# Expert stages: the down products' second round and the release of their buffers placed ahead of the next group's gate products, and the branch hints placed elsewhere

## The chip, the core and the metric

One core of one Trainium2 chip runs one program. Time is device microseconds of one execution; a comparison is made between medians of runs taken on the same chip. Engines are named as in the profile: PE (TensorE matmuls), PEld (TensorE weight loads, issued by the same sequencer), DVE (VectorE), ACT (ScalarE), POOL (GpSimd), SP (SyncE, which here only issues DMAs). A q behind the name (PEq, SPq) is the engine's sequencer.

## What is computed

Two blocks on 256 tokens of width 1024, in float32. The first block has two layers, each an attention (differential attention, then a latent attention called mla) followed by a hierarchical mixture of 64 experts; the second block is a mixer and a gated MLP. The change touches the expert stages alone:

```python
weights = g_w * (e_w / jnp.sum(e_w, axis=-1, keepdims=True))      # two experts per token, of one group of eight
combine = jnp.einsum('tk,tke->te', weights, jax.nn.one_hot(expert_id, N_EXPERTS, dtype=jnp.float32))
def body(e, acc):
    hid = jax.nn.silu(t @ w_gate[e]) * (t @ w_up[e])               # 1024 -> 256, twice
    return acc + combine[:, e, None] * (hid @ w_down[e])           # 256 -> 1024
out = lax.fori_loop(0, N_EXPERTS, body, jnp.zeros_like(t))
```

All 64 experts' weights (three matrices of 1 MB each) are read from HBM once per layer, about 201 MB a layer.

## The kernel before

**Groups.** `moe(i, held)` handles layer i's 64 experts in 16 groups of four. Each expert has 32 slots (CAP). For a group, `gather_half` (L905) picks the tokens of the four experts by products with a one-hot matrix, in two halves; `expand` (L946) makes the gate products ("g") and the up products ("u") of the four experts side by side in one PSUM tile; `hidden` (L959) applies silu and multiplies; `hidden_T` transposes; `down_mm` (L974) makes the down products into two PSUM tiles; `weighted` (L988) scales them by the routing weight and splits them in two parts, on ACT and DVE; `scatter` (L1000) spreads them to the 256 tokens by products with the scatter matrix and DVE adds to x (L1007).

**Overflow.** If an expert of the group has more than 32 tokens, the next 32 are done in a second round: behind `tc.If(n > CAP)` labelled further (L1083) the kernel gathers them and makes their gate and up products, and behind a second `tc.If` labelled beyond (L1047) their down products and scatter (`down_more`, L1009). Inside it stands a further branch for third and later rounds (`rounds`, L1030). In this input that happens in group 1 and group 15 of layer 0 and in group 11 of layer 1. Where it doesn't happen, each engine takes the branch over the body.

**Order on PE.** PE's and SP's programs follow the order of the source (`manual_schedule`); ACT, DVE and POOL are ordered by the framework. In the iteration of group g the source has: down products of group g-1, gate products of g, scatter of g-1, beyond of g-1, release of D (the down weights' buffers) of g-1, up products of g, hidden, further of g, release of the gate and up buffers of g, scatter matrix of g, gather half 0 of g+1, transposes of g's hidden, gather half 1 of g+1. Group 15 is written out behind the loop.

**Hints.** `hint` (L1040) places an instruction on PE's sequencer that names a branch by its label and says it will likely be taken, behind a given product. The hint of beyond g-1 stands behind the last down product of g-1, that of further g behind the first up product of g. The branches of group 15 have none. `at` is the list of the last products, from which the place is taken.

**Buffers.** Class `Regions` has 16 buffers of 1 MB in SBUF. In an expert stage one holds the normalised tokens `h`, so 15 are for weights: 12 of a group and 3 of the next. The weights are loaded by one DMA each, issued by SP in the order gate, up, down (four each) group by group. A release (`reg.done`) lets the next transfers be issued, and they wait on the engines' semaphores for it. A release of D lets one down and three gate transfers go, a release of gate and up the next gate, four up and three down. SP keeps at most eight transfers under way. `reg.want(n)` keeps n buffers free for what follows.

Of the kernel before, what the change touches and what calls it, by code (L numbers as in the profile page):

```python
# [18 lines left out]
P = 128  # L19
# [220 lines left out]
def tile_model(ctx: ExitStack, tc: tile.TileContext, a: dict, out: bass.AP, stop: int = 6):  # L240
# [541 lines left out]
    def moe(i, held):  # L782
# [114 lines left out]

        def one_hot(rks, ov=False):

            gm = view(ov4[0], (T, 4, 32)) if ov else t1((T, 4, 32))  # L900
            for t in range(T):
                V.tensor_tensor(gm[:, t], sl4, rks[:, t, :, None].to_broadcast([P, 4, 32]), op=ALU.is_equal)
            return gm

        def gather_half(gm, xg, hb):  # L905

            pg = sc_ps()
            for k4 in range(4):
                for t in range(T):
                    PE.matmul(pg[:, ts(k4, P)], lhsT=h[:, t, 4 * hb + k4, :], rhs=gm[:, t].rearrange("p a b -> p (a b)"),  # L910
                              start=(t == 0), stop=(t == 1))
            V.tensor_tensor(xg[hb], pg.rearrange("p (k n) -> p k n", k=4),  # L912
                            gain[:, 4 * hb:4 * hb + 4, None].to_broadcast([P, 4, P]), op=ALU.mult)
# [30 lines left out]
        at = []  # L944

# [20 lines left out]
        def hidden_T(hd, ov=False):  # L966
            pt = at_ps()
            for k in range(2):
                PE.transpose(pt[:, ts(k, P)], hd.rearrange("p (q k) -> p k q", k=2)[:, k, :], ident)
            hT2 = view(ov4[1], (2, P)) if ov else t1((2, P))  # L970
            V.tensor_copy(hT2, pt[:, 0:256].rearrange("p (k n) -> p k n", k=2))
            return hT2
# [15 lines left out]
        def weighted(pys, hf, ws, ov=False, tables=False):  # L988
# [5 lines left out]
            ins = split_to(y[0], y[1], pys[hf], ws)  # L994
            if tables:
                with tc.issue_after(ins):
                    exp_log()
# [61 lines left out]
        last = None  # L1059
        with tc.manual_schedule(engines={ET.PE}):  # L1060
            for g in range(15):
                n = nc.values_load(cnt[0:1, g:g + 1], min_val=0, max_val=256) if g else None
                if g:
                    n_, hT2, sc, more = last
                    pys = down_mm(g - 1, hT2)
                    hint("beyond", g - 1, at[-1])
                    ys = [weighted(pys, hf, sc[1]) for hf in range(2)]
                pgu = ad_ps()
                expand(g, "g", pgu, xg)
                if g:  # L1070
                    for hf in range(2):
                        scatter(hf, sc[0], ys[hf])
                    beyond(g - 1, n_, more)
                    done(g - 1, "d")
# [3 lines left out]
                if g:  # L1078
                    hint("further", g, at[0])
# [16 lines left out]
                gather_half(gm, xg, 0)  # L1096
                hT2 = hidden_T(hd)
# [5 lines left out]
            n_, hT2, sc, more = last  # L1103
            pys = down_mm(14, hT2)
            hint("beyond", 14, at[-1])
            ys = [weighted(pys, hf, sc[1]) for hf in range(2)]
            pgu = ad_ps()
            expand(15, "g", pgu, xg)
            for hf in range(2):
                scatter(hf, sc[0], ys[hf])  # L1110
            beyond(14, n_, more)
            done(14, "d")
            pgu_o = mm_ps()
            with tc.If(n > CAP):
                xg_o, sc_o = further(15)
                expand(15, "g", pgu_o, xg_o)
            expand(15, "u", pgu, xg)
            hd = hidden(pgu)
            sc = scatter_matrix(15, gm)
            hT2 = hidden_T(hd)  # L1120
            with tc.If(n > CAP):
                expand(15, "u", pgu_o, xg_o)
                more = (hidden_T(hidden(pgu_o, True), True), sc_o)
            done(15, "g", "u")
            beyond(15, n, more)

            pys = down_mm(15, hT2)
            for hf in range(2):
                scatter(hf, sc[0], weighted(pys, hf, sc[1], tables=hf == 0))
        reg.want((7, 9)[i])  # L1130
        done(15, "d")
# [454 lines left out]
```

## Time and profile before

| what | value |
|---|---|
| median of 3 runs | 1635.39 us (1633.1 to 1638.16) |
| the profiled execution | 1631.57 us |
| its span, first to last instruction | 1629.8 us |
| mean granted TensorE clock | 0.919 |
| PE busy | 1342.7 us, 82% of the span |
| DVE, ACT busy | 691.8 us, 434.5 us |
| DMA | 513.14 MB, mean 315 GB/s |
| expert stages, by their first and last hidden | 170.8 to 638.7 us and 789.3 to 1245.0 us |

The page cuts the span into 40 slices of 40.7 us. In its DMA row a 9 says that the 16 DMA engines were busy 90% or more. PE's busy share counts matmuls whose ends are modelled, and is high in most slices, whether or not PE sets the pace; who waits for whom is read from the waits and the timeline. A sequencer hands instructions out ahead of the engine that runs them, so a branch can stand before the end of the product in front of it. A row of busy time by stretch holds the stretch, its length, then for PE, PEld, DVE, ACT and POOL the busy us and the number of instructions, then the granted clock as a share of full speed, the DMA share and GB/s.

### The profile page before, as it was taken

The numbers are of one execution on the slowest core, as the hardware profiler recorded it, in microseconds if no ns is written. First come the engines' busy times: TensorE is split into PE (matmuls) and PEld (weight loads), VectorE is DVE, ScalarE is ACT, GpSimd is POOL, SyncE is SP. The second block draws the span as 40 slices with busy tenths as digits, with TensorE's granted clock in tenths as the row PEclk, the third lists the DMA queues.
The fourth block names the chain that finished last, engine by engine and source line by source line (L and its number), as shares of the span: only waits on it lengthen the run. The fifth ranks groups of instructions, "written<-read, shape, count | busy, mean of one in ns | idle before, by whom it ended". The sixth has DMA issues, their size and how long they took to land. (4 is left out here: it accounts for less than half of the span.)

```text
span 1629.8 us, 26706 instructions
## 1 busy us (share of the span) xinstructions
PE 1342.7 (82%) x10695; PEld 927.9 (57%) x10695; DVE 691.8 (42%) x1630; ACT 434.5 (27%) x946; POOL 54.1 (3%) x69
## 2 busy tenths in 40 slices
PE   7998987777677777998877677778777899999996
PEld 6766654443354444776643454545442656599996
DVE  6875232222222223775322222222322754477776
ACT  5764010000000001774000000000001543455555
POOL 2100000000000000120000000000000010000001
PEclk9998999889878899999988989899888999999998
DMA  9377889999999998244999999999899764475410
GB/s 365 127 262 322 334 343 419 419 419 418 417 397 416 418 418 337 93 144 167 392 417 403 418 419 418 419 418 393 341 418 379 285 235 159 149 270 189 171 37 27
DMA packets 112810, 513.14 MB, mean 315 GB/s; under 512 B 13955, under 2 KB 41283, under 8 KB 61344
## 3 DMA queue, kind: packets, MB, share of 16 engines
q1 hardware_dynamic: 111296, 508.14, 78.5%
q8 instruction: 160, 2.62, 0.7%
q0 software_dynamic: 1024, 1.41, 0.3%
q14 instruction: 106, 0.87, 0.1%
q10 hardware_dynamic: 224, 0.10, 0.0%
HBM read 508.56 MB, written 1.05 MB: 313 GB/s over the span
## 5 line engine op out<-in xcount | busy, mean ns | idle before, releaser
L955 PE MATMUL ad<-R,t 128*32 128x256 f32 x4352 | 327.0, 421 | 101.4 <-DMA R<-in_moe_w_up_dram 42.2
L955 PEld LDWEIGHTS ad<-R,t 128*32 128x32 f32 x4352 | 171.1, 120 | 260.3 <-issue 87.6
L910 PE MATMUL sc<-t,R 128*128 128x128 f32 x1120 | 176.1, 323 | 18.2 <-issue 12.0
L910 PEld LDWEIGHTS sc<-t,R 128*128 128x128 f32 x1120 | 167.5, 237 | 20.6 <-issue 17.2
L1007 DVE TENSOR_TENSOR x<-x,mm 128x512 f32<-128x512 f32 x140 | 90.0, 684 | 149.0 <-PE mm L1004 149.0
L982 PE MATMUL mm<-R,t 128*32 128x512 f32 x1120 | 135.4, 625 | 9.5 <-PEq L1047 5.0
L961 ACT ACTIVATE t<-ad 128x256 f32<-128x256 f32 x34 | 13.0, 383 | 481.7 <-PE ad L955 481.7
L963 DVE TENSOR_TENSOR t<-t,ad 128x256 f32<-128x256 f32 x34 | 14.3, 421 | 254.4 <-ACT t L961 254.4
L409 ACT ACTIVATE t<-mm,ws 128x512 fp32r<-128x512 f32 x64 | 44.0, 687 | 263.1 <-PE mm L982 263.1
L912 DVE TENSOR_TENSOR t<-sc,ffng 128x512 f32<-128x512 f32 x70 | 48.4, 692 | 134.6 <-PE sc L910 134.6
L400 DVE TENSOR_TENSOR R<-R,R 128x1024 fp32r<-128x1024 f32 (+3 forms) x78 | 93.2, 1198 | 27.4 <-ACT R L399 26.1
L400 DVE TENSOR_TENSOR t<-R,t 128x1024 fp32r<-128x1024 f32 (+3 forms) x76 | 88.7, 1171 | 23.6 <-ACT t L399 23.4
L410 DVE SCALAR_TENSOR_TENSOR t<-mm,ws,t 128x512 fp32r<-128x512 f32 x64 | 48.0, 751 | 104.3 <-ACT t L409 77.5
L399 ACT ACTIVATE R<-R 128x1024 fp32r<-128x1024 f32 (+3 forms) x78 | 78.7, 1014 | 50.8 <-PE ad L417 15.1
L934 PE MATMUL at<-con,t 128*128 128x128 f32 x70 | 16.6, 323 | 85.5 <-PEq L1083 73.9
L1004 PE MATMUL mm<-t,t 128*128 128x512 f32 x256 | 77.6, 422 | 11.1 <-DVE x L1007 10.2
L399 ACT ACTIVATE t<-R 128x1024 fp32r<-128x1024 f32 (+3 forms) x76 | 76.4, 1008 | 37.8 <-PE ad L416 15.3
L982 PEld LDWEIGHTS mm<-R,t 128*32 128x32 f32 x1120 | 35.0, 114 | 82.9 <-issue 77.5
L1004 PEld LDWEIGHTS mm<-t,t 128*128 128x128 f32 x256 | 43.1, 188 | 45.6 <-DVE x L1007 22.8
L934 PEld LDWEIGHTS at<-con,t 128*128 128x128 f32 x70 | 7.9, 155 | 99.7 <-issue 89.5
L415 PE MATMUL mm<-R,R 128*128 128x512 f32 (+3 forms) x139 | 56.4, 408 | 3.3 <-ACT R L399 2.6
L416 PE MATMUL mm<-R,R 128*128 128x512 f32 (+3 forms) x139 | 55.4, 399 | 0.0
(448 smaller groups left out, 2263.8 us busy)
## 6 DMA issues: line engine op xcount, KB each, us to landing
R<-in_moe_w_gate_dram SPq DMA_DIRECT2D x128, 1024.0 KB, 15.2
R<-in_moe_w_up_dram SPq DMA_DIRECT2D x128, 1024.0 KB, 15.8
R<-in_moe_w_down_dram SPq DMA_DIRECT2D x128, 1024.0 KB, 19.8
R<-in_w_ada_dram SPq DMA_DIRECT2D x24, 1024.0 KB, 7.7
R<-in_w_up_dram SPq DMA_DIRECT2D x22, 1024.0 KB, 6.3
R<-in_diff_w_in_dram SPq DMA_DIRECT2D x12, 1024.0 KB, 15.0
R<-in_w_down_dram SPq DMA_DIRECT2D x11, 1024.0 KB, 5.5
R<-in_w_in_dram SPq DMA_DIRECT2D x8, 1024.0 KB, 7.7
```

What stands on the lines that cost most here:

```text
L399: S.activation(hi, w, AF.Copy)
L400: V.tensor_tensor(lo, w, hi.bitcast(F32), op=ALU.subtract)
L409: first = S.activation(hi, src, AF.Copy, scale=scale)
L410: V.scalar_tensor_tensor(lo, src, scale, hi.bitcast(F32), op0=ALU.mult, op1=ALU.subtract)
L415: PE.matmul(acc, lhsT=lt[0], rhs=rt[0], start=start, stop=False, **kw)
L416: PE.matmul(acc, lhsT=lt[0], rhs=rt[1], start=False, stop=False, **kw)
L910: PE.matmul(pg[:, ts(k4, P)], lhsT=h[:, t, 4 * hb + k4, :], rhs=gm[:, t].rearrange("p a b -> p (a b)"), start=(t == 0), stop=(t == 1))
L912: V.tensor_tensor(xg[hb], pg.rearrange("p (k n) -> p k n", k=4), gain[:, 4 * hb:4 * hb + 4, None].to_broadcast([P, 4, P]), op=ALU.mult)
L955: mm = PE.matmul(pgu[32 * j:32 * j + 32, co:co + 256], lhsT=xg[k // 4][:, k % 4, 32 * j:32 * j + 32], rhs=w, start=(k == 0 and co == 0), s ...
L982: mm = PE.matmul(py[32 * j:32 * j + 32, :], lhsT=hT2[:, k, 32 * j:32 * j + 32], rhs=ws[j][:, k, ts(hf, 512)], start=(k == 0), stop=(k == 1))
L1004: PE.matmul(pos[t], lhsT=sc[:, ts(t, P)], rhs=y[part], start=(part == 0), stop=(part == 1))
L1007: V.tensor_tensor(xs, xs, pos[t], op=ALU.add)
```

## The change

In the loop, `down_mm`, `weighted`, `beyond` and the release of D become one function `close(g)`, which stands ahead of the gate products of g+1; the scatter stays behind the gate products. The hint of further g stands behind the last gate product of g, ahead of the scatter. The hint of beyond g stands behind the first half of the gather of g+1. In group 15 the overflow's gather stands ahead of the gate products, its gate and up products both behind hidden, under a branch with a label and a hint; beyond 15 stands behind the first round's down products, and has a hint; the activation table for the next stage (`exp_log`) is loaded ahead of the last scatter and no longer inside `weighted`; `reg.want` stands ahead of the last group's down products.

```diff
--- before.py
+++ after.py
@@ -895,6 +895,9 @@
         ov4 = [t15() for _ in range(4)]
         r2 = sb([P, T, 4], "r2")
 
+
+        at = []
+
         def one_hot(rks, ov=False):
 
             gm = view(ov4[0], (T, 4, 32)) if ov else t1((T, 4, 32))
@@ -907,8 +910,9 @@
             pg = sc_ps()
             for k4 in range(4):
                 for t in range(T):
-                    PE.matmul(pg[:, ts(k4, P)], lhsT=h[:, t, 4 * hb + k4, :], rhs=gm[:, t].rearrange("p a b -> p (a b)"),
-                              start=(t == 0), stop=(t == 1))
+                    mm = PE.matmul(pg[:, ts(k4, P)], lhsT=h[:, t, 4 * hb + k4, :],
+                                   rhs=gm[:, t].rearrange("p a b -> p (a b)"), start=(t == 0), stop=(t == 1))
+            at.append(mm.ins)
             V.tensor_tensor(xg[hb], pg.rearrange("p (k n) -> p k n", k=4),
                             gain[:, 4 * hb:4 * hb + 4, None].to_broadcast([P, 4, P]), op=ALU.mult)
 
@@ -941,8 +945,6 @@
             V.tensor_copy(ws, ptr[:, 256:257])
             return sc, ws
 
-        at = []
-
         def expand(g, nm, pgu, xg):
 
             ws = [reg.get(("moe", i, g, nm, j)) for j in range(4)]
@@ -966,7 +968,8 @@
         def hidden_T(hd, ov=False):
             pt = at_ps()
             for k in range(2):
-                PE.transpose(pt[:, ts(k, P)], hd.rearrange("p (q k) -> p k q", k=2)[:, k, :], ident)
+                mm = PE.transpose(pt[:, ts(k, P)], hd.rearrange("p (q k) -> p k q", k=2)[:, k, :], ident)
+            at.append(mm.ins)
             hT2 = view(ov4[1], (2, P)) if ov else t1((2, P))
             V.tensor_copy(hT2, pt[:, 0:256].rearrange("p (k n) -> p k n", k=2))
             return hT2
@@ -985,16 +988,13 @@
                 pys.append(py)
             return pys
 
-        def weighted(pys, hf, ws, ov=False, tables=False):
+        def weighted(pys, hf, ws, ov=False):
             if ov:
                 y = ovy
             else:
                 room = t4((2, 512), F32R)
                 y = [room[:, 0, :], room[:, 1, :]]
-            ins = split_to(y[0], y[1], pys[hf], ws)
-            if tables:
-                with tc.issue_after(ins):
-                    exp_log()
+            split_to(y[0], y[1], pys[hf], ws)
             return y
 
         def scatter(hf, sc, y):
@@ -1057,26 +1057,30 @@
 
         gm, xg = gather(rk[:, :, 0:4])
         last = None
+
+        def close(g):
+
+            n, hT2, sc, more = last
+            pys = down_mm(g, hT2)
+            ys = [weighted(pys, hf, sc[1]) for hf in range(2)]
+            beyond(g, n, more)
+            done(g, "d")
+            return sc, ys
+
         with tc.manual_schedule(engines={ET.PE}):
             for g in range(15):
                 n = nc.values_load(cnt[0:1, g:g + 1], min_val=0, max_val=256) if g else None
                 if g:
-                    n_, hT2, sc, more = last
-                    pys = down_mm(g - 1, hT2)
-                    hint("beyond", g - 1, at[-1])
-                    ys = [weighted(pys, hf, sc[1]) for hf in range(2)]
+                    sc, ys = close(g - 1)
                 pgu = ad_ps()
                 expand(g, "g", pgu, xg)
                 if g:
+                    hint("further", g, at[-1])
                     for hf in range(2):
                         scatter(hf, sc[0], ys[hf])
-                    beyond(g - 1, n_, more)
-                    done(g - 1, "d")
                 else:
                     done(0, "g")
                 expand(g, "u", pgu, xg)
-                if g:
-                    hint("further", g, at[0])
                 hd = hidden(pgu)
                 more = None
                 if g:
@@ -1094,41 +1098,39 @@
                 sc = scatter_matrix(g, gm)
                 gm, xg = one_hot(rk[:, :, 4 * g + 4:4 * g + 8]), slots()
                 gather_half(gm, xg, 0)
+                hint("beyond", g, at[-1])
                 hT2 = hidden_T(hd)
                 gather_half(gm, xg, 1)
                 last = (n, hT2, sc, more)
 
             reg.want(8)
             n = nc.values_load(cnt[0:1, 15:16], min_val=0, max_val=256)
-            n_, hT2, sc, more = last
-            pys = down_mm(14, hT2)
-            hint("beyond", 14, at[-1])
-            ys = [weighted(pys, hf, sc[1]) for hf in range(2)]
+            sc, ys = close(14)
+            with tc.If(n > CAP):
+                xg_o, sc_o = further(15)
             pgu = ad_ps()
             expand(15, "g", pgu, xg)
+            hint("further", 15, at[-1])
             for hf in range(2):
                 scatter(hf, sc[0], ys[hf])
-            beyond(14, n_, more)
-            done(14, "d")
-            pgu_o = mm_ps()
-            with tc.If(n > CAP):
-                xg_o, sc_o = further(15)
-                expand(15, "g", pgu_o, xg_o)
             expand(15, "u", pgu, xg)
             hd = hidden(pgu)
+            with tc.If(n > CAP, label=f"further{i}_15"):
+                pgu = ad_ps()
+                for nm in "gu":
+                    expand(15, nm, pgu, xg_o)
+                more = (hidden_T(hidden(pgu, True), True), sc_o)
+            done(15, "g", "u")
             sc = scatter_matrix(15, gm)
             hT2 = hidden_T(hd)
-            with tc.If(n > CAP):
-                expand(15, "u", pgu_o, xg_o)
-                more = (hidden_T(hidden(pgu_o, True), True), sc_o)
-            done(15, "g", "u")
-            beyond(15, n, more)
-
-            pys = down_mm(15, hT2)
+            hint("beyond", 15, at[-1])
+            last = (n, hT2, sc, more)
+            reg.want((7, 9)[i])
+            sc, ys = close(15)
+
+            exp_log()
             for hf in range(2):
-                scatter(hf, sc[0], weighted(pys, hf, sc[1], tables=hf == 0))
-        reg.want((7, 9)[i])
-        done(15, "d")
+                scatter(hf, sc[0], ys[hf])
         reg.give(rh)
 
 
```

## Rows read from the trace of the kernel before

**Rows 1.** busy time by stretch; last columns PE clock, DMA share, GB/s

```profile
196.00:206.00 10.00, 8.80 (x142) 5.61 (x142) 1.88 (x7) 1.15 (x3) 0.00 (x0) 1.00 0.82 320
...
220.00:232.00 12.00, 10.72 (x97) 6.52 (x92) 4.43 (x7) 1.37 (x2) 0.00 (x0) 0.86 0.50 192
...
256.00:400.00 144.00, 107.92 (x1018) 64.97 (x1010) 33.75 (x71) 10.70 (x20) 0.00 (x0) 0.89 1.01 418
...
1140.00:1156.00 16.00, 12.84 (x116) 5.82 (x112) 6.56 (x10) 1.55 (x3) 0.00 (x0) 1.00 0.62 231
```

**Rows 2.** waits, PE's weight loads: us in total, times, longest

```profile
PEld ad L955 <- DMA R<-in_moe_w_up_dram: 59.5, 36, 4.0
...
PEld ad L955 <- DMA R<-in_moe_w_gate_dram: 38.8, 25, 3.4
```

**Rows 3.** timeline at two second rounds: start, us, what, [idle]

```profile
203.73 23.32 SPq L122 DMA_DIRECT2D R<-in_moe_w_down_dram  x4
...
213.07 3.64 PE L955 MATMUL ad<-R,t 128*32 128x256 f32 x64
...
219.29 3.64 PE L982 MATMUL mm<-R,t 128*32 128x512 f32 x32
...
227.04 5.43 PE L955 MATMUL ad<-R,t 128*32 128x256 f32 x64 [0.44 <-PEq L1030]
...
1150.39 1.27 PE L955 MATMUL ad<-R,t 128*32 128x256 f32 x17 [0.44 <-PEq L1030]
...
1159.44 0.66 PE L934 MATMUL at<-con,t 128*128 128x128 f32 x2 [3.67 <-PEq L1083]
```

**Rows 4.** waits of PE: us in total, times, longest

```profile
PE at L934 <- PEq L1083: 73.9, 19, 5.3
...
PE ad L955 <- PEq L1047: 12.6, 11, 5.4
```

**Rows 5.** hints (L1582), branches: ns min/median/max, first and last start

```profile
L1582 PEldq BRANCH_PREFETCH_HINT  x2: 36/38/41, 403.1 to 421.8; - x2
...
L1083 PEldq COMPARE_BRANCH  x1: 6078/6078/6078, 408.3 to 408.3; - x1
...
L1582 PEldq BRANCH_PREFETCH_HINT  x1: 31/31/31, 556.5 to 556.5; - x1
...
L1083 PEldq COMPARE_BRANCH  x1: 2880/2880/2880, 564.8 to 564.8; - x1
```

**Rows 6.** timeline of PE in one group: gather half 0, then down

```profile
415.71 3.26 PE L910 MATMUL sc<-t,R 128*128 128x128 f32 x16
...
420.93 3.64 PE L982 MATMUL mm<-R,t 128*32 128x512 f32 x32
```

**Rows 7.** layer 0, end of experts: timeline, branch L1030 (ns)

```profile
640.58 3.64 PE L982 MATMUL mm<-R,t 128*32 128x512 f32 x32 [0.52 <-DVE t L971]
...
651.79 6.32 PE L982 MATMUL mm<-R,t 128*32 128x512 f32 x32 [3.91 <-DVE R L400]
...
661.97 1.28 DVE L1007 TENSOR_TENSOR x<-x,mm 128x512 f32<-128x512 f32 x2
...
L1030 PEldq COMPARE_BRANCH  x6: 192/282/3907, 225.9 to 1150.1; - x6
```

**Rows 8.** busy time by stretch: last down products of layer 0

```profile
651.80:658.10 6.30, 6.30 (x33) 1.63 (x33) 0.75 (x1) 1.97 (x2) 1.37 (x6) 0.57 0.29 94
```

**Rows 9.** layer 1, end of experts: timeline, last branch, last down transfer

```profile
1221.07 14.21 SPq L122 DMA_DIRECT2D R<-in_moe_w_down_dram  x4
...
1252.04 6.57 PE L982 MATMUL mm<-R,t 128*32 128x512 f32 x32 [5.01 <-PEq L1047]
...
1262.08 1.28 DVE L1007 TENSOR_TENSOR x<-x,mm 128x512 f32<-128x512 f32 x2 [0.54 <-PE mm L1004]
...
L1047 PEldq COMPARE_BRANCH  x1: 4397/4397/4397, 1247.2 to 1247.2; - x1
...
R<-in_moe_w_down_dram SPq DMA_DIRECT2D x1, 1024.0 KB, 13.5
```

## Prediction

> **What bounds the kernel now.** I read the slices of the page first: in both expert stages the transfer rate stands flat at its highest, and the reader is to see the few slices in which it dips. Then the table by stretch: from 256 to 400 us the DMA engines are busy 1.01 of the time at 418 GB/s, while PE is busy three quarters [rows 1]. The weights set the pace, and PE waits for them: 98.3 us over 32 groups, 3.1 us a group [rows 2]. Work that is only moved or shortened on PE inside these stretches is worth nothing. What counts is every stretch in which the DMA engines run dry, and the two ends of the stages, where the last weights are in and PE works alone.
>
> Dry stretches [rows 1]: 220 to 232 us at 0.50 (6.0 us lost), 196 to 206 us at 0.82 (1.8 us), 1140 to 1156 us at 0.62 (6.1 us). The first and last are the groups with more than 32 tokens on one expert (group 1 of layer 0, group 11 of layer 1). In the timeline [rows 3] SP is held on the last of four down transfers from 203.73 us for 23.32 us: it needs a D buffer of group 1, and these are given back only behind the second round, which ends just ahead of 227.04.
>
> **The change part by part.**
>
> *Second round and release ahead of the next gate products.* Nothing is added to the work, the order changes. Group 1, layer 0 [rows 3]: gate and scatter stand between first down (213.07 is where gate starts) and second down (219.29), 6.2 us. Without them the buffers come free 6.2 us sooner, near 220.8. The second round itself takes 219.29 to 227.04, 7.7 us, and I leave that: its PSUM tiles now follow straight on the first down's, whose readers are ACT and DVE, but the second tile alone could wait, under 1 us. Four transfers follow a release (one down, three gate), some 10 us of the DMA engines' time at 418 GB/s. They would start before the engines are dry. The next eight need the gate and up buffers of group 2, and these do not come sooner than today, as the PE work up to there is the same. So of the 6.0 us not all returns. In layer 0 the earlier start puts the four in line behind running transfers; I take 3.5 us, bounds 0 and 6.0. In layer 1 the release stands just ahead of 1150.39, and would be 6.2 us sooner, near 1144; the four are moved by 1154. The next release stands just ahead of 1159.44 [rows 3], behind a further branch that PE waits 3.67 us for, and comes at 1156 to 1158 with the hint moved (below). Some 3 us stay dry: of 6.1 us I take 3, bounds 0 and 6.1. Neither term can fall below nothing, as no buffer in these groups comes free later than today but by the charge below. Groups without a second round: D comes free sooner too, the transfers go out sooner, and queue behind others that already fill the engines. Nothing.
>
> What is queued behind: on ACT and DVE the branch now precedes the scatter's additions to x; these engines pass a branch without a visible wait. On SP four DMA issues wait for an earlier semaphore; POOL only branches. The order of want and done moves no transfer ahead of another.
>
> *Hints.* Every branch over a second round costs PE a fetch. At the further branch (L1083) PE stands 73.9 us in 19 groups, 3.9 each; at the beyond branch (L1047) hardly, 12.6 us in 11 [rows 4]. The hints show why [rows 5]. A hint at 403.1 stands 5.2 us ahead of the branch at 408.3, which takes 6.08; a hint at 556.5 stands 8.3 us ahead of one at 564.8, which takes 2.88. Both add to 11.2 or 11.3 us from hint to go-ahead, with 6.1 as the most. So I price a branch at 11.2 us less its lead, at most 6.1. Further: the hint moves from the first up product to the last gate product, ahead of the scatter (2.6 us, the end of gate to 219.29 [rows 3]) and of the sequencer's own lead. The lead grows to 7.8 to 9.7 us, the branch falls to 1.5 to 3.4, and as it is handed out some 2 us before the up products end, PE stands 0 to 1.5 us in place of 3.9. Beyond: its hint moves behind the first half of the gather, and the branch right behind the down products. The half gather ends at 418.97, down at 424.57 [rows 6]: lead 5.6 us, branch 5.6. The old hint behind the last down product was handed out at 421.8 [rows 5], so the sequencer is 2.8 us ahead of PE, and PE stands 2.8 us, bounds 0.8 and 3.5. Net per group: minus 2.4 to 3.9, plus 2.8. In the paced stretches the 3.1 us of weight waits [rows 2] cover it either way. Not covered is group 0 of layer 0, whose follower is not yet paced: PE gets 2.8 us later to group 1's buffers, and the dry spell at 196 to 206 us grows by that. I charge 2 us, bounds 0 and 3.5. The same in layer 1 has queued transfers as cover.
>
> [...]
>
> *Last group, layer 0* (it has a second round) [rows 7]. Today: second down at 640.58, its round to 647.88, 3.91 us of idleness, first down 651.79 for 6.32 us, its scatter to 663.25, the end of the last addition to x. Total 22.7 us. The view puts the idle time down to DVE; I read it as the branch over further rounds (L1030), of which one of six took 3.907 us and the median 0.28. In that first down the granted clock was 0.57, most of it at the lower of the two levels, behind that idleness [rows 8]; the second down took 3.64 for the same products. After: down 3.6, second round 7.3, scatter 2.6 and the last pair of additions 1.3, and the hint that beyond 15 now gets covers the L1030 branch, as its target lies right behind. Sum 14.8, gain 7.9. The overflow's gather (5 to 6 us of PE) moves ahead of gate, where it waits for no weights, but the beyond stall of group 14 (2.8) precedes it, and the overflow's gate products move behind the up products. I take these as even. Term: 8 us, bounds 5 (the fetch stays or the clock does) and 11 (the gather's move counts).
>
> *Last group, layer 1* (none) [rows 9]. The last down transfer is issued near 1235, the end of SP's row, and lands 13.5 us later, near 1248.4. PE starts down at 1252.04 only, behind a beyond branch of 4.40 us, and takes 6.57 us; x is complete at 1263.36. After: down from 1248.4, 3.6 us, to 1252.1. Then the beyond branch: short lead, 4.4 to 6.1 us from about 1249.3, so scatter starts at 1253.7 to 1255.4, and takes 3.9 with additions: x at 1257.6 to 1259.3. The new skip of the overflow's two products in front of it (about 3 us by the same law) lies largely beside the wait for the last transfer. Gain 4 to 6: 5 us, bounds 1 (the skip uncovered) and 7.
>
> Sum: 3.5 + 3 + 8 + 5 - 2 = 17.5 us. The profiled execution took 1631.57 us, so 1614.1. The runs shown have their median at 1635.39, 3.8 us above it; on that base 1617.9.
>
> **The rivals.**
>
> *Only the ends count.* If the buffers of the group behind an overflow release late, the dry time is moved, not removed: the first two terms and the charge fall away, 13 us stay, 1622. For: those eight transfers hang on unchanged PE work. Against: a whole dry spell of 6 us closes while others open by 3.
>
> *Given back.* The stages behind the experts wait for their own weights or for ACT and DVE, and the ends' 13 us dissolve: 3 to 5 us stay, 1630 to 1632. For: behind layer 1 the next weights follow the last expert weights at once, so the engines do not rest. Against: behind layer 0 their share is 0.29 by 652 us [rows 8].
>
> *The change does not do what it says.* The early release finds SP held for another buffer, and the hints are late: 1635. Little speaks for it, as the SP row of [rows 3] ends with the release; it shares a chance with the former.
>
> *The beyond fetch sets the pace (slower).* If hints are worth nothing, each of 28 groups gets the stall at beyond and keeps the one at further. One such wait is in the trace, 5.4 us [rows 4]. Less the cover of 3.1, 2.3 us x 28 is 64 us, less the gains of 17.5: 47 slower, 1682. It decides from a stall of 3.7 us a group (3.1 + 17.5/28) with the further stall unchanged; from there to 1682 lies its range. For: leads get no longer than 5.6 us at beyond. Against: the further stall shrinks by the same law, and 2.8 us of the fetch lie beside running products.
>
> **How the numbers follow.** Forecast 0.66, own range 1609 to 1625. Only the ends 0.14 (1622). Given back or without effect 0.11 (1630 to 1636). Slower 0.09. The range holding 8 in 10: low end 1608, nearly all terms near their upper bounds; high end 1630, which takes in the second case. About 0.3%, 4.9 us, is what a measurement of this kernel can tell from no change; 1630.5 is then the border. Faster 0.81: the first two cases and a little of the third. Same 0.11, slower 0.08.
>
> **What the changed profile would show.** Right: the DMA share from 220 to 232 us above 0.8, SP's hold shorter than 20 us; stall at L1083 under 1.5 us a group and a new one of 1 to 3.5 at the beyond branch; in layer 0's end no 3.9 us branch, and the last down at 3.6 us; in layer 1's end down beginning with the last transfer. Wrong: PE's waits for weights near nothing and the rate in the middle slices under 410 GB/s, so that the fetch sets the pace; or x complete earlier at the experts' end with the next expert stage, or the kernel's end, no earlier.

## The result, and the profile after

| | before | after |
|---|---|---|
| median of 4 runs | 1636.68 us | 1656.50 us |
| lowest to highest | 1633.10 to 1638.16 | 1654.46 to 1658.24 |
| profiled execution / its span | 1631.57 / 1629.8 us | 1657.52 / 1655.7 us |
| mean granted clock of PE | 0.919 | 0.911 |

The ratio is 1.0132, 95% interval 1.0103 to 1.016: 20 us slower, where 18 us faster was forecast and the range ended at 1630.

**Where the time went.** Three marks that stand in both traces cut the span in four: the end of the last addition to x in each layer (DVE L1007, [rows 7, 9]) and the start of layer 1's first hidden (ACT L961 before, L963 after). Stretches, in us:

| stretch | before | after | difference | forecast |
|---|---|---|---|---|
| start to x of layer 0 complete | 663.25 | 659.10 | -4.2 | -9.5 |
| to the first hidden of layer 1 | 126.04 | 148.47 | **+22.4** | 0 |
| to x of layer 1 complete | 474.08 | 464.53 | -9.5 | -8 |
| to the end of the span | 366.42 | 383.60 | **+17.2** | 0 |

The marks of after, from its timeline (start, us, what, idle before it):

```profile
657.81 1.29 DVE L1007 TENSOR_TENSOR x<-x,mm 128x512 f32<-128x512 f32 x2 [0.71 <-PE mm L1004]
...
807.57 0.38 ACT L963 ACTIVATE t<-ad 128x256 f32<-128x256 f32 x1 [14.53 <-PE ad L957]
...
1270.82 1.29 DVE L1007 TENSOR_TENSOR x<-x,mm 128x512 f32<-128x512 f32 x2 [0.69 <-PE mm L1004]
```

The two stretches that hold the expert stages, which the change was about, became 13.7 us shorter. The two between and behind them, which compute attention, mixer and MLP and in which no line was edited, became 39.6 us longer. What differs in them is ScalarE. First the groups of table loads of after, then those of before (line, engine, operation, count | busy us, mean ns of one):

```profile
L350 ACT ACT_TABLE_LOAD x11 | 14.1, 1283 | 0.2
L351 ACT ACT_TABLE_LOAD x11 | 14.1, 1283 | 0.2
L335 ACT ACT_TABLE_LOAD x3 | 3.8, 1283 | 1.8 <-issue 1.7
```

```profile
L335 ACT ACT_TABLE_LOAD x4 | 5.1, 1283 | 1.8 <-issue 1.7
L1461 ACT ACT_TABLE_LOAD x1 | 1.3, 1283 | 0.2 <-DVE t L1459 0.2
```

With two loads for Silu in either (L963 after, L961 before) and three more single loads in after (L616, L1343, L1463) that is 30 against 7. L350 and L351 are the logarithm and the exponential of `rsqrt`. L335 is `exp_log`, the load of one table by its name. In before it is tied to an ACT instruction of the last group (`issue_after`) and stands at 656.20 and 1256.44 us, behind the last Silu of each expert stage; before's trace has no load at L350 or L351. In after it hangs on nothing. Timeline of ACT in before, behind the experts of layer 0, then in after, at the program's start and behind the same experts:

```profile
656.20 1.28 ACT L335 ACT_TABLE_LOAD   x1
...
672.24 0.20 ACT L350 ACTIVATE rs_a<-ms_u 128x2 f32<-128x2 f32 x1
...
673.07 0.19 ACT L351 ACTIVATE rs<-rs_a 128x2 f32<-128x2 f32 x1
```

```profile
8.44 1.28 ACT L335 ACT_TABLE_LOAD   x1
...
669.09 1.28 ACT L350 ACT_TABLE_LOAD   x1
670.38 0.20 ACT L350 ACTIVATE rs_a<-ms_u 128x2 f32<-128x2 f32 x1
...
671.44 1.28 ACT L351 ACT_TABLE_LOAD   x1
672.73 0.20 ACT L351 ACTIVATE rs<-rs_a 128x2 f32<-128x2 f32 x1
```

ACT's order isn't written by hand (PE's and SP's are), and the load that depends on nothing is found at the front of the program: it runs at 8.44 us, where it is useless. Of the call's two places, one in each layer, the trace has this one load; behind the experts it has none. From there to the load at 1639.31 us, 11 times in all, a load of 1.28 us stands at a logarithm and another at the exponential behind it. One load served both where that table was asked for (before: the load at 656.20 and none at L350 or L351); where it wasn't (after), each of the two got a load of its own.

What the loads do to the stretch between the layers, by the tables of busy time (after, then `tied`, the experiment below that has 7 loads; us, PE, PEld, DVE, ACT, POOL, clock, DMA share, GB/s):

```profile
659.00:682.00 23.00, 21.66 (x129) 19.79 (x128) 17.73 (x44) 19.51 (x46) 1.34 (x2) 1.00 0.41 138
682.00:706.00 24.00, 17.09 (x79) 14.37 (x77) 12.95 (x36) 20.38 (x62) 4.65 (x6) 0.86 0.14 45
706.00:735.00 29.00, 25.58 (x109) 20.03 (x108) 18.81 (x64) 21.32 (x65) 3.92 (x4) 0.82 0.22 64
...
sum 149.00, PE 125.58 PEld 100.24 DVE 83.11 ACT 91.29 POOL 12.89; mean PE 25.12 PEld 20.05 DVE 16.62 ACT 18.26 POOL 2.58
```

```profile
657.00:680.00 23.00, 23.00 (x138) 21.45 (x136) 19.00 (x49) 18.29 (x52) 1.34 (x2) 0.97 0.42 138
680.00:700.00 20.00, 18.28 (x94) 14.54 (x92) 16.25 (x52) 16.33 (x64) 4.67 (x6) 1.00 0.17 54
700.00:726.00 26.00, 26.00 (x143) 21.72 (x142) 21.70 (x67) 19.18 (x63) 5.74 (x6) 1.00 0.49 164
...
sum 127.00, PE 117.51 PEld 95.43 DVE 82.93 ACT 73.04 POOL 12.92; mean PE 23.50 PEld 19.09 DVE 16.59 ACT 14.61 POOL 2.58
```

PE is the engine at work here. ACT is busy 18.3 us more (91.29 against 73.04); PE stands 13.9 us longer (149.00 - 125.58 against 127.00 - 117.51), and is busy 8.1 us more with the same products, at a granted clock of 0.86 and 0.82 in two stretches where `tied` has 1.00. So 14 more loads (L350 and L351, seven each), 18.0 us of their own, cost 22 us: most of it PE's waiting, the rest a lower clock in the stretches in which it waits.

### The profile page after: what moved, and what is told of

The parts are those of the page before. It is cut to its first block, busy times and chain, and to the rows that moved or that the text cites. A ratio compares the mean times of both kernels' runs of the same rounds, so it can differ in the third digit from the quotient of the medians.

```text
span 1655.7 us, 26872 instructions
## 1 busy us (share of the span) xinstructions
PE 1350.8 (82%) x10695; PEld 921.9 (56%) x10695; DVE 692.5 (42%) x1630; ACT 464.2 (28%) x969; POOL 53.9 (3%) x69
## 5 line engine op out<-in xcount | busy, mean ns | idle before, releaser
L957 PE MATMUL ad<-R,t 128*32 128x256 f32 x4480 | 339.6, 431 | 129.3 <-PEq L1047 42.4
L1007 DVE TENSOR_TENSOR x<-x,mm 128x512 f32<-128x512 f32 x140 | 90.0, 684 | 256.3 <-PE mm L1004 256.3
L913 PE MATMUL sc<-t,R 128*128 128x128 f32 x1120 | 166.3, 311 | 12.3 <-issue 6.3
L963 ACT ACTIVATE t<-ad 128x256 f32<-128x256 f32 x35 | 13.4, 383 | 546.7 <-PE ad L957 546.7
L913 PEld LDWEIGHTS sc<-t,R 128*128 128x128 f32 x1120 | 157.4, 225 | 15.3 <-DVE t L905 7.8
L985 PE MATMUL mm<-R,t 128*32 128x512 f32 x1120 | 129.7, 601 | 1.8 <-DVE t L974 1.0
L399 ACT ACTIVATE R<-R 128x1024 fp32r<-128x1024 f32 (+3 forms) x78 | 78.5, 1012 | 45.2 <-PE ad L417 15.4
L399 ACT ACTIVATE t<-R 128x1024 fp32r<-128x1024 f32 (+3 forms) x76 | 76.4, 1010 | 43.5 <-PE ad L416 18.3
L938 PE MATMUL at<-con,t 128*128 128x128 f32 x70 | 15.3, 302 | 60.1 <-PEq L1087 37.5
L415 PE MATMUL mm<-t,R 128*128 128x512 f32 (+3 forms) x139 | 55.7, 402 | 3.3 <-ACT junk L1238 3.3
## 6 DMA issues: line engine op xcount, KB each, us to landing
R<-in_diff_w_in_dram SPq DMA_DIRECT2D x12, 1024.0 KB, 14.6
```

Of the source, the lines that this page charges most:

```text
L399: S.activation(hi, w, AF.Copy)
L415: PE.matmul(acc, lhsT=lt[0], rhs=rt[0], start=start, stop=False, **kw)
L913: mm = PE.matmul(pg[:, ts(k4, P)], lhsT=h[:, t, 4 * hb + k4, :], rhs=gm[:, t].rearrange("p a b -> p (a b)"), start=(t == 0), stop=(t == 1))
L957: mm = PE.matmul(pgu[32 * j:32 * j + 32, co:co + 256], lhsT=xg[k // 4][:, k % 4, 32 * j:32 * j + 32], rhs=w, start=(k == 0 and co == 0), s ...
L985: mm = PE.matmul(py[32 * j:32 * j + 32, :], lhsT=hT2[:, k, 32 * j:32 * j + 32], rhs=ws[j][:, k, ts(hf, 512)], start=(k == 0), stop=(k == 1))
L1007: V.tensor_tensor(xs, xs, pos[t], op=ALU.add)
```

## The experiments

All kernels, with the four stretches' differences from before (us, from each trace by the marks above) and the time. A trace is one execution, and executions of one kernel lie up to 14 us apart (midonly, 1635.84 to 1649.99), so 2 us in these columns mean nothing; pad64 has two executions, the others four to ten.

| kernel | median us | ratio to before, interval | loads | to x, layer 0 | between | experts 1 | behind |
|---|---|---|---|---|---|---|---|
| after | 1656.5 | 1.0132 (1.0103 to 1.016) | 30 | -4.2 | +22.4 | -9.5 | +17.2 |
| tied | 1621.6 | 0.9906 (0.9883 to 0.9929) | 7 | -5.8 | -0.1 | -7.9 | +3.6 |
| loose | 1671.6 | 1.0212 (1.0182 to 1.0241) | 30 | +2.5 | +21.0 | +3.6 | +14.6 |
| l0tied | 1631.2 | 0.9978 (0.9961 to 0.9995) | 16 | -4.5 | -0.1 | -11.9 | +10.5 |
| lastonly | 1626.5 | 0.995 (0.9926 to 0.9974) | 7 | -7.6 | -1.1 | -1.4 | +3.1 |
| midonly | 1642.9 | 1.004 (1.0022 to 1.0059) | 7 | +3.3 | -1.5 | +3.7 | +0.3 |
| oldhints | 1661.3 | 1.0156 (1.0113 to 1.0199) | 7 | +9.0 | -1.4 | +15.5 | +3.5 |
| hintonly | 1639.5 | 1.0023 (1.0001 to 1.0045) | 7 | +0.6 | 0.0 | +0.9 | +1.3 |
| pad32 | 1622.4 | 0.9935 (0.9893 to 0.9977) | 7 | -8.7 | -0.8 | -7.4 | +6.4 |
| pad64 | 1619.7 | 0.9895 (0.9843 to 0.9947) | 7 | -3.7 | -0.4 | -11.3 | +3.6 |
| hint15 | 1619.5 | 0.9903 (0.9868 to 0.9938) | 7 | -5.2 | +0.6 | -11.7 | +0.6 |
| earlier | 1612.4 | 0.9863 (0.9827 to 0.99) | 7 | -16.3 | +0.7 | -9.5 | +3.8 |

### The table loads: tied, loose, l0tied

**tied**, against after:

```diff
-            exp_log()
             for hf in range(2):
                 scatter(hf, sc[0], ys[hf])
+                if hf == 0:
+                    tie = S.activation(junk((1,)), x[:, 0, 0:1], AF.Copy)
+                    with tc.issue_after(tie.ins):
+                        exp_log()
```

> The changed kernel with one edit: the table load at the end of an expert stage (exp_log) hangs on a one-element ACT copy of x behind the first half of the last scatter, so that it can't leave that place. Theory 1 (tables): the trace of the changed kernel has 30 table loads where that of before has 7, and between the end of the layer-0 experts and the first hidden of layer 1 it loses 22.9 us, behind layer 1 another 17.2. With 7 loads again both come back, about 40 us: 1656.5 - 40 = 1617 (1613 to 1621), 1.2% under the kernel before. Rival A: only the loads' own time comes back, 23 x 1.283 = 29.5 us: 1627. Rival B: the stages between the experts lost their time to something else that the change moved (weights that are fetched later, the order of the last scatter): then the loads are a side show and the time stays above 1645. In the expert stages nothing should change against the changed kernel: the last weights of layer 0 at 628 to 632 us, x complete about 28.5 us later.

Measured 1621.57 us, 34.9 under after and 14.2 under before. The 22.4 us between the layers came back whole, of the 17.2 behind layer 1 13.6. Rival B falls; the time lies between theory 1 and rival A.

**loose**, against before:

```diff
             pys = down_mm(15, hT2)
+            exp_log()
             for hf in range(2):
-                scatter(hf, sc[0], weighted(pys, hf, sc[1], tables=hf == 0))
+                scatter(hf, sc[0], weighted(pys, hf, sc[1]))
```

(and the tied call in `weighted` goes.)

> The kernel before with that edit alone in the other direction: exp_log stands ahead of the last scatter and hangs on nothing, all else as before. Theory 1 (tables): 30 loads instead of 7, and the kernel is 40 us slower, 1677 (1672 to 1681). Rival A (own time only): 1666. Rival B (the moves did it): no more than 1645.

Measured 1671.59, 35.8 over before, from one line moved. That is within its range. Both ways round the 23 loads cost 35 us, 1.5 us each for 1.283 of their own. Table loads alone turned a gain of 14 us into a loss of 20.

**l0tied**, against tied: `if hf == 0 and i == 0` ahead of the tie, and a bare `exp_log()` in layer 1.

> The kernel tied with the table load held in its place in layer 0 alone; in layer 1 it hangs on nothing, as in the changed kernel: 16 loads, the 9 more all behind layer 1. If each stage pays for its own loads, the stages between the layers stay as in tied (first weights of layer 1 landed at 775, x of layer 1 at 1250 us) and the stretch behind layer 1 becomes 13 us longer (9 loads at 1.5 us in the changed kernel and loose): 1635 (1631 to 1639). If only the loads' own 1.283 us count: 11.5 us, 1633. If the cost of the loads came from one place in layer 0 alone: 1622.

Measured 1631.15, inside the range. Each stage does pay for its own loads: between the layers nothing, behind layer 1 6.9 us over tied. The price of the 9 loads is 9.6 us by the two medians and 11.8 us by the two ratios to before; with these intervals it can't be told from the loads' own 11.5 us, nor from the 13 us expected.

### What the rest of the change is worth: lastonly, midonly

**lastonly** is before with everything from `reg.want(8)` on as in tied, but the hint of beyond 14 stays behind its down products; **midonly** is before with the loop over groups 0 to 14 (`close`, both hints) as in after.

> The kernel before with the last group alone as in the changed kernel (from the close of group 14 on, its second gather ahead of its gate products, beyond 15 behind its first down products), with the tied table load; groups 0 to 13 and their hints as before. From the traces of before and after: from the last weights to x complete 34.8 us became 28.6 in layer 0, and 22.5 became 17.2 in layer 1. Theory: both gains belong to the last group and stand alone: 1636.7 - 6.2 - 5.3 = 1625 (1621 to 1629). Rival: they need what the rest of the change does (a later close frees nothing by itself): within 3 us of before, 1634 to 1640. My prediction had 8 + 5 for them, which would be 1624.

Measured 1626.48: 8.2 us by the ratio, most of it layer 0's (-7.6). In layer 1 the gain hardly came (-1.4). Two branches took 6.2 us each there, beyond 14, which stands right behind its hint, and beyond 15. No run separated them, but the trace has PE start its last down products at 1240.38 us, 0.1 us behind the landing of the last weights, so beyond 14 did not hold them up; they took 6.20 us, where such products took 3.64 in before at a granted clock of 1.00 (219.29 us [rows 3]), and the scatter came another 2.05 us later, behind beyond 15.

> The kernel before with groups 0 to 14 alone as in the changed kernel (D, second round and release ahead of the gate products, both hints moved), the last group and the table load as before. The landings of the weights in the two traces: layer 0 loses 3.0 us between group 0 and group 2, layer 1 gains 4.8 around group 11, the rest is level. Theory: 1636.7 + 3.0 - 4.8 = 1635 (1631 to 1638). The prediction had gains of 3.5 and 3 and a charge of 2 here: 1632. Rival: the moves in the loop cost nothing and gain 4.8 alone, if the loss in layer 0 is chance: 1632 with layer-0 landings level with before.

Measured 1642.89, 7 us slower than before and 8 above the theory. By the landings of the weights the term of group 11 is there (some 5 us), the loss in group 1 too (some 1.3 us). New is the end, where the change's loop meets the old last group. Branches over beyond at the end of midonly's layer 1, and what PE waited (L1050 is its line of that branch):

```profile
L1050 PEldq COMPARE_BRANCH  x2: 6038/6575/7112, 1232.3 to 1250.1; - x2
...
1238.99 1.88 PE L957 MATMUL ad<-R,t 128*32 128x256 f32 x11 [5.68 <-PEq L1121]
...
1257.65 5.35 PE L985 MATMUL mm<-R,t 128*32 128x512 f32 x24 [7.73 <-PEq L1050]
```

Two such branches in a row, both on the path that ends the stage. So the parts do not add: -8 and +7 alone, -14 together.

### The hints: oldhints, hintonly, pad32, pad64

**oldhints**, against tied:

```diff
             pys = down_mm(g, hT2)
+            if hinted:
+                hint("beyond", g, at[-1])
...
-                    hint("further", g, at[-1])
...
                 expand(g, "u", pgu, xg)
+                if g:
+                    hint("further", g, at[0])
...
-                hint("beyond", g, at[-1])
```

(`hinted` is set for the groups 0 to 14.)

> The kernel tied with the two hints of groups 1 to 14 back where the kernel before has them (beyond behind the last down product, further behind the first up product); all that was moved stays moved. It asks what the hints are worth, and why the branch over the rounds (L1030) stalls 4.0 to 4.7 us in group 1 of layer 0 in the changed kernel, tied and midonly (0.4 in before, loose and lastonly), which is the place where layer 0 loses 1.5 to 3 us. Theory E (the hint comes too early and its fetch is lost): with the hint behind down the stall goes to 0 to 2 us, the further hint's lead shrinks, and the layer-0 start is 1 to 3 us better. Theory P (it is the place of the branch's target in the program, which this edit leaves where it is to within a hint): the stall stays at 4 us. The lead law of the prediction makes the stall of a beyond branch that is taken 6 us in every group, beside 3 to 4.5 us now: nothing in the stretches that the transfers pace. Time: 1621.6 and 0 to 4 us more or less, 1618 to 1626; if the hints' places carried the gain of tied, it would fall back to 1630 or more.

Measured 1661.26: 40 us over tied, far outside what I wrote. The waits of PE (us in total, times, longest), tied and then oldhints, and oldhints' rate in the middle of layer 0:

```profile
PE ad L957 <- PEq L1047: 49.2, 26, 3.8
PE at L938 <- PEq L1087: 38.8, 13, 4.4
```

```profile
PE ad L957 <- PEq L1047: 97.2, 26, 4.0
PE at L938 <- PEq L1090: 59.2, 19, 4.9
...
256.00:400.00 144.00, 97.02 (x944) 57.92 (x944) 32.41 (x66) 9.25 (x17) 0.00 (x0) 0.83 0.96 392
```

With the branch right behind its hint PE stands 3.7 us at beyond in each of 26 groups, ahead of D's release, and 392 GB/s stand in place of 418 [rows 1]. That is the mechanism of the prediction's slower rival, "the beyond fetch sets the pace", with its place and its threshold of 3.7 us a group; it costs 26 us against before, where that rival had 47. It did not happen in after, whose rate over the same 144 us is 418 GB/s: tied and oldhints differ in the hints' places alone. With the old places the same order of the work loses to before, with the new ones it gains 14 us.

Of the two theories on L1030, P held here: in group 1 of layer 0 the branch stalled 3.87 us, behind a lead of 9.1 us (a lead is the time from the hint to the branch), and in group 11 of layer 1 it now stalled too, 3.77 us.

**hintonly** is before with the two hints of after.

> The kernel before with the two hints alone moved to their places in the changed kernel (further behind the last gate product, beyond inside the gather), nothing else. Theory E: the branch over the rounds in group 1 of layer 0 stalls 4 us as in the changed kernel, for its hint comes as early: 2 us slower than before, 1638. Theory P: no stall there, as in before. By the lead law the further branch stalls less (its lead grows by the scatter and the up products, some 5 us, so 0 to 1.5 us instead of 3.9), hidden beside the transfers: 1636 and 0 to 3 us less.

Measured 1639.48, 0.2% over before. PE's wait at further fell from 73.9 us [rows 4] to 47.8 in the trace, and the time did not follow; that the transfers cover the branches is the likely reason. The branch L1030 stalled 3.85 us, as theory E had it, and the time is near its 1638.

**pad32** and **pad64**, against tied:

```diff
+    pad = at_ps()
+    for _ in range(32):
+        PE.matmul(pad[0:1, 0:1], lhsT=one, rhs=one, start=True, stop=True)
```

> The kernel tied with 32 one-column products (64 instructions) ahead of the first PE instruction, where PE waits 6.3 us for its first data; the rest of PE's program is the same but stands 64 instructions further on. Theory E: nothing changes, the branch over the rounds stalls 4.0 us in group 1 of layer 0, 0.4 in group 11 of layer 1 and 5.0 in group 15 of layer 0, as in tied. Theory P: at least one of these three changes by more than 2 us, and other unhinted jumps do too. Time 1621.6, 5 us either way.

> As pad32 with 64 one-column products (128 instructions). Theory E: the three stalls as in tied, 4.0, 0.4 and 5.0 us. Theory P: at least one of them changes by more than 2 us, and not by the same as in pad32. Time 1621.6, 5 us either way.

The branch over further rounds (ns, min/median/max of six) in after, pad32 (L1034) and pad64 (L1034):

```profile
L1030 PEldq COMPARE_BRANCH  x6: 187/320/4682, 220.1 to 1162.3; - x6
```

```profile
L1034 PEldq COMPARE_BRANCH  x6: 176/272/438, 219.0 to 1132.3; - x6
```

```profile
L1034 PEldq COMPARE_BRANCH  x6: 191/338/5451, 221.7 to 1139.9; - x6
```

64 instructions of padding took both stalls away, 128 did not. In group 1 the lead from the hint is 13.6 to 13.8 us in all three, so there the stall changed with the padding and not with the lead; at the end of layer 0 the lead differs too (12.8, 15.4 and 11.2 us). So theory E does not hold alone: with the same order and lead, a shift of the program decides whether this branch stalls. It also has the long leads against it: in earlier (below) this branch takes 0.45 us in group 1, behind a lead of 31 us. Theory P does not hold alone either, since hintonly moved little but a hint. Why the shift does that was not shown. What the stall cost is read from SP's row in group 1, after and then pad32:

```profile
204.02 21.26 SPq L122 DMA_DIRECT2D R<-in_moe_w_down_dram  x4
```

```profile
202.87 17.30 SPq L122 DMA_DIRECT2D R<-in_moe_w_down_dram  x4
```

D comes free at 225.3 in after and at 220.2 in pad32, where the prediction had it near 220.8; the hold is 4.0 us shorter. By the landings of the weights, layer 0 loses some 3.0 us against before from group 1 on in after and some 1.7 in tied, and gains 4 in pad32. To x, layer 0 gains 8.7 us in pad32, 3.7 to 5.8 in after, tied and pad64.

### More lead for the beyond hint: earlier, hint15

**earlier**, against tied (hint15: the last group alone):

```diff
                 expand(g, "u", pgu, xg)
+                hint("beyond", g, at[-1])
                 hd = hidden(pgu)
...
                 gather_half(gm, xg, 0)
-                hint("beyond", g, at[-1])
```

> The kernel tied with the beyond hint of every group moved still further forward: behind the last up product of the same group, ahead of the further branch. In tied the lead of this hint is 3.6 to 8 us and the beyond branch stalls 2.4 to 6.0 us; oldhints, with 0.1 us of lead, stalled 6.0 in every group and took 40 us more. Theory A (the lead is what counts): the lead becomes 9 to 14 us, the stalls 0 to 2 us. In the stretches that the transfers pace that is worth nothing, at the start of layer 1, in its groups 12 to 14 and at its end 1 to 3 us each: 1616 (1611 to 1621). Theory B (the further branch that is taken in between throws the fetched code away): the stalls are 6 us in every group as in oldhints, D's release is late again and the time is 1650 to 1662.

Measured 1612.43 us, 1.4% under before and the fastest here. The branch over beyond, 32 times (ns, min/median/max), in tied, oldhints and earlier:

```profile
L1047 PEldq COMPARE_BRANCH  x32: 78/3904/6196, 175.4 to 1239.0; - x32
```

```profile
L1047 PEldq COMPARE_BRANCH  x32: 78/6039/6339, 177.6 to 1277.4; - x32
```

```profile
L1047 PEldq COMPARE_BRANCH  x32: 86/366/6132, 176.0 to 1228.8; - x32
...
L1030 PEldq COMPARE_BRANCH  x6: 181/330/463, 219.5 to 1126.5; - x6
```

Theory A holds for the median, 0.37 us. It does not hold throughout: of the 29 branches over beyond that are taken, 14 still take 2.2 to 6.1 us, behind leads of 6.9 to 14.2 us, and 15 take 0.3 to 0.5 behind leads of 8.6 to 15.0. So more lead helps, and is not all that counts. The 9 us that earlier gains on tied all stand in layer 0 (-16.3 against -5.8), where L1030 stalls nowhere; pad32, with no stall there either and the hint where tied has it, reaches -8.7, so how much of the gain is the hint's was not separated. At the places in layer 1 that I named little came (-9.5 against -7.9).

> The kernel tied with the beyond hint of the last group alone moved in that way. The beyond branch of the last group of layer 1 stalls 2.4 us in tied (4.4 in before, 6.2 in lastonly, 5.6 in pad32) after 3.6 us of lead. Theory A: 0 to 1 us of stall, x of layer 1 complete 2 us sooner: 1619.5, not to be told from tied by the time, to be told by the row of the branch. Theory B: 6 us of stall and x 3.6 us later, 1625.

Measured 1619.52. The branch took 0.34 us in place of 2.38, and that brought nothing. In the end of layer 1, hint15 and then tied, what the scatter waits for behind down is the same:

```profile
1237.89 3.62 PE L985 MATMUL mm<-R,t 128*32 128x512 f32 x26 [1.53 <-DMA R<-in_moe_w_down_dram]
1243.29 1.39 PE L1004 MATMUL mm<-t,t 128*128 128x512 f32 x5 [1.78 <-DVEq L1047]
```

```profile
1238.87 5.12 PE L985 MATMUL mm<-R,t 128*32 128x512 f32 x26 [1.16 <-DMA R<-in_moe_w_down_dram]
1245.77 1.39 PE L1004 MATMUL mm<-t,t 128*128 128x512 f32 x5 [1.78 <-DVEq L1047]
...
1244.82 0.75 DVE L410 SCALAR_TENSOR_TENSOR t<-mm,ws,t 128x512 fp32r<-128x512 f32 x1 [1.03 <-ACTq L1047]
...
L1047 DVEq COMPARE_BRANCH  x1: 56/56/56, 1244.8 to 1244.8; - x1
```

The scatter waits 1.78 us for DVE's semaphore either way. That is not DVE's branch, which takes 0.06 us, but `weighted` of the second half, which ACT (0.69 us) and DVE (0.75 us, the row at 1244.82) do first; PE's own branch lies beside it. Of the 2.5 us by which x is complete sooner in hint15, 1.0 is an earlier start of down and 1.5 the shorter time of the down products, 3.62 against 5.12 us.

## Why the prediction was wrong

**The step that failed is one that it does not have.** The change list holds "the activation table for the next stage is loaded ahead of the last scatter", and the prediction costs every other edit but not this one: its sum, 3.5 + 3 + 8 + 5 - 2, puts the edit at nothing, without a reason. The code and the trace of before had what was needed to ask: a call tied by `issue_after`, and one load of 1.28 us that serves every logarithm and exponential behind an expert stage. Missing term: +35 us, measured in both directions (tied -34.9, loose +35.8). Without it the kernel is at 1621.6 us, 3.7 from the forecast of 1618 and inside its range. That closeness is part luck: in tied the term of group 1 has the other sign, and that of group 11 is 1.9 us larger than forecast.

**The terms, by tied, which is after without the loads.**

- *Ends, 8 and 5 us.* Layer 0: from the first of the two down products to x took 22.7 us [rows 7] and takes 20.6 in tied (from 636.87 to 657.42), with a wait of 4.86 us at L1030; the forecast was 14.8. "The hint that beyond 15 now gets covers the L1030 branch" was wrong: with a lead of 11.2 us (635.65 to 646.87) it stalled 5.04. In earlier, where it does not stall, the same stretch is 16.9 us (630.05 to 646.94). Layer 1: down now begins with its last transfer, as forecast; between down and scatter PE now waits 1.8 us for `weighted` at the branch's semaphore, where the sum had 1.6 to 3.3 for PE's own branch and let ACT and DVE pass without a visible wait: a fitting size, for the wrong reason. From the landing of the last weights to x, the ends gain 6.2 and 5.2 us in after, 6.3 and 4.2 in tied, within their bounds.
- *Group 1 of layer 0, 3.5 us less a charge of 2.* Wrong in sign in after, where the weights land 3.0 us later behind it: the share from 220 to 232 us is 0.68, not above 0.8 (0.94 in pad32), and SP's hold 21.26 us, not under 20. The release was forecast right but for 4.5 us at L1030, a branch that had cost 0.44 us before [rows 3] and was costed at nothing. In pad32, without it, the hold is 17.30 us and the weights land 4 us sooner. The charge came about as priced: from 196 to 206 us the share is 0.67 in after, 0.82 before, 1.5 us.
- *Group 11 of layer 1, 3 us.* Right: the dry spell [rows 1, the last one] comes 18 us later in after, and its share is 0.99 there in place of 0.62. By the landings of its weights, layer 1 gains 5.0 us around it in after and 4.9 in tied, within the bounds of 0 and 6.1.
- *Hints.* The further branch: 37.5 us in 11 groups in place of 73.9 in 19 [rows 4]. That is 3.4 us each where it is paid, forecast 0 to 1.5: fewer groups pay, and those pay nearly as before. Beyond: 42.4 us in 25, 1.7 each, forecast 2.8, bounds 0.8 and 3.5, so this size was right. The law (11.2 us less the lead, at most 6.1) was read from two branches. It holds at its upper end, some 6.0 us in every group of oldhints whose branch is taken; in after 23 of the 29 beyond branches that are taken add to 8.5 to 11.4 us with their lead, the others to less. It fails with longer leads: in after twelve further branches take 3.1 to 6.3 us behind leads of 6.7 to 12.1, 12.5 to 15.5 us in sum, and others at such leads take 0.3 to 0.6; L1030 in after and midonly's beyond 14 (6.0 us behind a hint 18 us earlier) pay all the same.

**The rivals.** The one on the slower side had the wrong cause: its rate test, under 410 GB/s, is not met in after (418) and is met in oldhints (392). "Given back" has a little in it: of the 13.8 us that tied has gained when x of layer 1 is complete, the stretch behind loses 3.6 (see below).

Busy time of after by stretch, the same of pad32, and the waits of PE in after:

```profile
220.00:232.00 12.00, 7.31 (x71) 3.92 (x71) 1.83 (x4) 0.00 (x0) 0.00 (x0) 0.72 0.68 243
...
256.00:400.00 144.00, 107.41 (x1014) 66.34 (x1010) 36.33 (x75) 10.70 (x20) 0.00 (x0) 0.87 1.01 418
1158.00:1174.00 16.00, 12.99 (x150) 7.27 (x147) 7.03 (x14) 1.07 (x2) 0.00 (x0) 1.00 0.99 389
```

```profile
220.00:232.00 12.00, 9.59 (x136) 5.71 (x136) 4.28 (x10) 0.38 (x1) 0.00 (x0) 1.00 0.94 373
```

```profile
PE ad L957 <- PEq L1047: 42.4, 25, 3.9
PE at L938 <- PEq L1087: 37.5, 11, 5.2
PE ad L957 <- PEq L1030: 5.1, 2, 4.5
PE mm L1004 <- PEq L1030: 3.4, 1, 3.4
```

## What to carry to other kernels

Cost every line of a diff, above all the one that looks like housekeeping: in this kernel an instruction that sets an engine's state and hangs on no data stayed where it works only while something tied it there, so ask of each such line what held it before and what holds it now. Count table loads in the profile of both kernels before reading anything else of ScalarE. A branch over a second round took 6.0 us here with its hint right ahead of it (oldhints, the median at beyond) and 0.37 us with its hint behind the up products (earlier, median), so a release that moves behind a branch must bring its hint along, far enough ahead; read from the trace which branches still pay, for a longer lead did not spare all of them (the longest in earlier took 6.13 us).

## What was unexpected of the hardware

**A clock that falls at one place.** Behind layer 1, tied loses 3.6 us although its instructions there are those of before. Most of it can be seen in one spot, some 140 us behind the end of the experts. Busy time by stretch, before and then tied:

```profile
1402.00:1406.00 4.00, 4.00 (x20) 2.55 (x19) 1.58 (x9) 1.30 (x5) 0.00 (x0) 1.00 0.00 0
```

```profile
1384.00:1388.00 4.00, 4.00 (x20) 2.39 (x18) 1.09 (x6) 1.28 (x2) 0.00 (x0) 1.00 0.80 262
1388.00:1392.00 4.00, 4.00 (x12) 1.88 (x10) 0.15 (x1) 1.61 (x6) 0.00 (x0) 0.59 0.00 0
1392.00:1396.00 4.00, 4.00 (x13) 3.00 (x12) 1.57 (x9) 0.29 (x1) 0.00 (x0) 0.56 0.00 0
```

PE is busy all the time in both, with the same work; in tied the granted clock is 0.59 and 0.56 in two stretches of 4 us, and PE was busy all through the 4 us in front of it at 1.00. lastonly, pad32, pad64, hint15 and earlier show such a dip among these products too (0.50 to 0.55 over 4 us), before and midonly none (1.00). It does not settle the stretch alone: hint15 has the dip and loses 0.6 us. That the same products at another moment get another clock is shown; why is not.

**A branch's price that hangs on its place.** With the same order and the same lead of its hint, L1030 took 4.0 us or 0.4 us in group 1 of layer 0, by 64 instructions of padding ahead of it. A study of one kernel can't tell an order that is 4 us better from one that lies better in the program; here it took copies with two amounts of padding.
